# A decoder layer in split fp32: one weight transfer merged, three small steps and a row load moved earlier

## The chip, the cores and the metric

The kernel runs on one core of a Trainium2 chip. The metric is the device time of one execution in microseconds. The core has a matrix engine (TensorE; PE in the rows, PEld for its weight loads), a vector engine (VectorE, DVE), a scalar engine (ScalarE, ACT), GpSimd (POOL) and a sync engine (SP) that issues most transfers. Each engine works through its own list of instructions in order; semaphores tie the lists together.

## The reference, cut to what matters

One layer of a decoder trunk on x of 512 tokens by 1024 channels, float32: a half-step feed-forward network, a mixer, and a second half-step feed-forward network. Each reads a normalised x and adds a normalised result back to it.

```python
def swiglu(x, w_gu, w_down):
    gate, up = jnp.split(x @ w_gu, 2, axis=-1)
    return (jax.nn.silu(gate) * up) @ w_down

x = x + 0.5 * rms_norm(swiglu(rms_norm(x, ffn1_pre_g[l]), ffn1_w_gu[l], ffn1_w_down[l]), ffn1_post_g[l])
y = hybrid_mixer(rms_norm(x, mix_pre_g[l]), ...)
x = x + rms_norm(y, mix_post_g[l])
x = x + 0.5 * rms_norm(swiglu(rms_norm(x, ffn2_pre_g[l]), ffn2_w_gu[l], ffn2_w_down[l]), ffn2_post_g[l])
```

The hidden width of a feed-forward network is 2816, that is 22 chunks of 128. The mixer runs a gated linear recurrence beside sliding-window attention; the change does not touch it.

## The kernel before, in words

**Split numbers.** Every product is done with a high and a low part of each operand. ScalarE casts the high part (names with `hi`, `hh`, `xh`, "cast" below), VectorE subtracts it from the original to get the low part (`lo`, `hl`, `xl`). Three matmuls (high by high, high by low, low by high) then stand for one. So each weight that TensorE uses first costs a transfer, a cast on ScalarE and a subtraction on VectorE.

**Weights.** `Weights` (object `W`) holds two lists in program order: raw transfers into 5 buffers (`NRAW`), and units (a cast and a low part). `W.take(ahead)` hands out the next unit and first calls `fill(1 + ahead)`, which makes sure that many units are cast and split; `W.cast(n)` only casts ahead. When the last unit of a raw buffer is split, the next transfer of the list is issued on SP's queue. So where `fill` and `cast` stand in the program is where their instructions stand in ScalarE's and VectorE's lists. Casts go into 6 buffers (`NWS`). `W.later(n, fn)` runs `fn` when n more units have been taken; `W.owed` puts loads of x in the place of weight loads.

**A feed-forward network.** The first chunks are done plainly (`classic`), the others in groups of four by a scheme with seven products instead of eight (`octo`: forms `b11`, `t3`, `t2`, `b21`, `t1`, `t4`, `b22`; `SevenDown` for the way back, which also runs seven products, from `a11` to `s1`). After a group its hidden values are moved from one layout to another by 32 small transfers, half on SP's queue and half on POOL's (`place`, `ha<-sqa` and `hb<-sqb` in the rows). FFN1 works on groups from chunk 4 to 19 and has chunks 20 and 21 left; FFN2 on groups from chunk 2 to 21. Partial sums go to memory (`yp_a`, `yp_b`) and are read back in the last group.

**The end of a network.** The last group's way back is done by blocks of 128 tokens (`Last`, tb 0 to 3): TensorE finishes the two 512-column halves (dh 0 and 1) of a block, VectorE adds the partial sums (the columns of dh 1 have the negative sign), ScalarE sums the squares. In FFN1 `boundary` then normalises the rows of block after block (`Rows`: `inverse` for root and reciprocal, `x_rows` for the new x, `xn` for the normalised row), transposes them on TensorE (`tp_r`), and starts the first products of the mixer (`an`) before the last block is through. The mixer's end and the start of FFN2 go through the same function (products `mn`). In FFN2's end the sum times the post-norm gain (`grow`, a row of 1024 broadcast to 128 partitions) is done on POOL for blocks 0 to 2, and VectorE finishes with a scale and an add of x (L1971) and SP writes out.

**Order of the work around the change.** `add_layer` lists the weight transfers; `last_order` gives those of the last group and the chunks left over, by (chunk, count, dh). In `boundary` ScalarE's list holds, before block 3 is handled, a first cast, a `W.fill(2)`, then the row steps of block 2 and 3, then `W.cast(4)`. At FFN2's start ScalarE's list holds the forms of the normalised x (`n2.forms`: sums on VectorE, casts on ScalarE, low parts on VectorE), then the gates of the two plain chunks (`hid.classic`: Silu, product, split), then the units of the first way back (`bd`), which `first_part` uses. The broadcast load of `grow` is issued on SP's queue after everything of the last group, the moves of hidden blocks among it. Small tiles of 2 KB a partition (`t2k`) share 41 buffers, so a load into one can have to wait until an earlier tile is done with.

Of the kernel before, what the change touches and what calls it, by code (L numbers as in the profile page):

```python
# [11 lines left out]
AF = mybir.ActivationFunctionType  # L12
# [3 lines left out]
P = 128  # L16
T = 512
NB = T // P
D = 1024
# [15 lines left out]
OCTO1, OCTO2 = (4, 20), (2, 22)  # L35
# [86 lines left out]
def tile_layer(ctx: ExitStack, tc: tile.TileContext, out: bass.AP, **ins: bass.AP):  # L122
# [15 lines left out]
    HALF_D = [slice(0, T), slice(T, D)]  # L138
# [21 lines left out]
    W = Weights()  # L160
    w1, w2, w_in, w_o = ins["ffn1_w_gu"], ins["ffn2_w_gu"], ins["w_in"], ins["w_o"]

    def load_raw(srcs, nk, w, name):
        raw = wpool.tile([P, nk * w], F32, tag="raw", name=f"raw_{name}", bufs=NRAW).rearrange("p (k c) -> p k c", k=nk)
        o = 0
        for src in srcs:
            n = src.shape[1]
            sync.dma_start(raw[:, :, o:o + n], src.rearrange("(k p) c -> p k c", p=P))
            o += n
        return raw  # L170
# [5 lines left out]
    def add_unit(r, part, nk, c, name, low=dve, negative=False):  # L176
        def two(t, like):
            return t.rearrange("p k (i d) -> p k i d", i=2) if len(like.shape) == 4 else t

        def cast(raw):  # L180
            x, (hi, lo) = part(raw), w_tiles(nk, c, name)
            if negative:
                act.activation(hi, x, AF.Copy, scale=-1.0)
            else:
                act.copy(two(hi, x), x)
            return hi, lo

        def take_low(raw, hi, lo):
            x = part(raw)
            if negative:  # L190
                dve.scalar_tensor_tensor(lo, x, -1.0, hi.bitcast(F32), op0=ALU.mult, op1=ALU.subtract)
                return
            low.tensor_sub(two(lo, x), x, two(hi.bitcast(F32), x))

        W.unit(r, cast, take_low)
# [122 lines left out]
    def add_down(wd, name, f, n, dh, negative=False):  # L318

        down_units(down_raw(wd, name, f, n, dh), name, f, n, dh, negative)  # L320
# [8 lines left out]
    def add_layer(w_gu, wd, name, classic, octo, done):  # L329

        groups = list(range(*octo, 4))
        for f in range(done, classic, 2):
            add_gate_up(w_gu, f, name)
        if classic == octo[0] and classic == CLASSIC1:
            for dh in range(2):
                add_down(wd, name, 0, classic, dh)
        for f in groups:
            if f == groups[-1]:
                for q in range(octo[1], FC, 2):
                    add_quad(w_gu, q, name)  # L340
            add_octo(w_gu, f, name, f < CLASSIC1 and (lambda: add_downs(wd, name, 0, 2)))
            if f > groups[0]:
                add_seven_down(wd, f - 4, name)
        for f, n, dh in last_order(groups[-1], FC):
            add_down(wd, name, f, n, dh, dh)

    for add in add_pair([w1[0, :, o + P:o + 2 * P] for o in (0, F)], KD, "second", (dve, pool)):
        add()
# [49 lines left out]
    for i in range(2):  # L398
        load_x(0, i)
        for o in (0, F):  # L400
            r = first_raw[o, i] = t2k(f"first{o}{i}").rearrange("p (k c) -> p k c", k=4)
# [36 lines left out]
    def preload(func):  # L438
        act.activation(dummy, eps, func)
# [222 lines left out]
    def row_pieces(gain):  # L662
        grow = [t2k(f"grow_{gain}{dh}") for dh in range(2)]
        for dh in range(2):
            sync.dma_start(grow[dh], ins[gain][0:1, dh * T:(dh + 1) * T].to_broadcast([P, T]))
        return grow
# [71 lines left out]
    def boundary(rows, produce, parts, turns, fills, ahead, name, beside=None):  # L738


        nxt = rows.nxt
        lower, upper = range(4), range(4, KD)
        chain = iter(())

        def advance(n):
            for _ in range(n):
                next(chain, None)

        for tb in range(NB - 1):
            for dh in range(2):  # L750
                ps = produce(tb, dh)
                for t in turns.get((tb, dh), ()):
                    rows.turn(t)
                if dh == 0:
                    advance(3)
                rows.piece(tb, dh, ps, parts and parts[tb, dh])
                W.fill(fills.get((tb, dh), 0))
            chain = rows.steps(tb)
            if tb < NB - 2:
                advance(ahead)  # L760
        ps = [produce(NB - 1, dh) for dh in range(2)]
        advance(1)
        rows.turned(nxt.high, 0, lower)
        advance(1)
        rows.turned(nxt.low, 0, lower)
        W.cast(1)
        rows.turned(nxt.high, 0, upper)
        advance(1)
        rows.turned(nxt.low, 0, upper)
        W.fill(2)  # L770
        advance(1)
        for dh in range(2):
            rows.piece(NB - 1, dh, ps[dh], parts and parts[NB - 1, dh])
        if nxt.xg:
            rows.turned(nxt.keep, 0, range(KD))
        xs, (l, r) = nxt.xs, (lambda t: nxt.half(t, 0), lambda t: nxt.half(t, 1))
        W.cast(4)
        ws, banks = [], []

        def one(n, part, xpart, stop=False):  # L780
            for w, b in zip(ws[n:], banks[n:]):
                for k in range(KD):
                    pe.matmul(l(b), w[part][:, k, :], l(xs[k][xpart]), start=k + part + xpart == 0, stop=stop and k == KD - 1)  # L783

        def more():
            ws.extend(W.take(0) for _ in range(2))
            banks.extend(bank(f"{name}n{len(banks)}") for _ in range(2))

        more()
        one(0, 0, 0)  # L790
        one(0, 0, 1)
        one(0, 1, 0, True)
        chain = rows.steps(NB - 1)
        advance(4)
        W.fill(2)
        rows.turn(2)
        more()
        one(2, 0, 0)
        one(2, 0, 1)
        rows.turn(3)  # L800
        for cs in (lower, upper):
            rows.turned(nxt.high, 1, cs)
            rows.turned(nxt.low, 1, cs)
        if nxt.xg:
            rows.turned(nxt.keep, 1, range(KD))
        one(2, 1, 0, True)
        W.fill(2)
        if beside:
            beside()
        k_high(ws, banks, xs, r, range(KD))  # L810
        k_low(ws, banks, xs, r)
        return banks
# [379 lines left out]
    banks = [bank(f"a_first{i}") for i in range(4)]  # L1192
# [127 lines left out]
    hid = Hidden("a", n1)  # L1320

    def hbm_parts(name):
        return {(tb, dh): hbm.tile([P, T], F32, name=f"yp_{name}{tb}{dh}") for tb in range(NB) for dh in range(2)}
# [39 lines left out]
    def octos(hid, f0, f1, in_hbm, early=None, beside=None):  # L1363

        order = ("a11", "+s3", "s3", "a12", "+s1", "+s2", "s2", "+s4", "s4")
        parts = {}
        for f in range(f0, f1, 4):
            last = f == f1 - 4
            if last:
                for q in range(f1, FC, 2):  # L1370
                    hid.quad(q, False, AHEAD)
                W.later(11, lambda: parts.update(read_parts(hid.name, in_hbm)))
                if beside:
                    W.later(13, beside)
            if f > f0:
                down = SevenDown(hid, f - 4)
                down.ahead(zip((6, 6, 7, 8, 9, 9, 10, 11, 12) if f == f0 + 4 else (1, 2, 3, 4, 5, 6, 7, 8, 9), order))
            hid.octo(f, None if f > f0 else early)
            if f == f0:
                placed(hid, (1, 2, 3, 4))  # L1380
                continue
            if last:
                whole = Whole(hid, f)
                placed(hid, (1, 1, 2, 2), (0, 2, 1, 3))
                for n, name in zip((6, 7), ("a11", "a12")):
                    W.later(n, whole.split, name)
            else:
                placed(hid, (3, 4, 5, 6))
            kept = down.run(by_tokens, lambda half, dh, i: (parts if last else in_hbm)[2 * half + i, dh], [["a22"], ["s1"]], last)
        return whole, parts, kept  # L1390
# [71 lines left out]
    def beside():  # L1462
        grow1.extend(row_pieces("ffn1_post_g"))
        load_gates()

    whole, parts, kept = octos(hid, *OCTO1, parts1, None, beside)
# [386 lines left out]
    n2 = Turned("f2", "ffn2_pre_g", True)  # L1853
# [53 lines left out]
            wo_product(tb, dh, k0, False, k0 == 2)  # L1907
        return wo_banks[tb][dh]

    banks = boundary(rows2, produce, None, {(2, 0): [0], (2, 1): [1]}, {(0, 0): 2, (1, 0): 2}, 2, "m", n2.forms)  # L1910
    x_rows.clear()

    hid = Hidden("b", n2)
    parts2 = hbm_parts("b")
    hs = hid.classic(2, banks, {})

    def first_part():
# [4 lines left out]
        W.later(8, n2.blocks)  # L1922

    f0, f1 = OCTO2[1] - 4, FC
    whole, parts, kept = octos(hid, *OCTO2, parts2, first_part)
    hs = whole.hs
    for i in range(2):
        load_rows(i, x_hbm, pool)
    preload(AF.Sqrt)
    grow = row_pieces("ffn2_post_g")  # L1930

    last = Last(f0, f1)
    for tb in range(NB):
        end = tb == NB - 1
        pieces = [(0, 0, T)] + ([(1, 0, T // 2), (1, T // 2, T)] if end else [(1, 0, T)])
        banks = [kept.get((tb, i)) or bank(f"ybl{tb}{i}") for i in range(len(pieces))]
# [64 lines left out]
```

## Time and profile before

| | |
|---|---|
| median of 3 runs | 835.74 us (834.51 to 838.97) |
| profiled execution | 837.13 us |
| its span in the trace | 835.4 us |
| granted TensorE clock, mean | 0.997 |
| TensorE busy | 819.9 us, 98% of the span |
| VectorE / ScalarE / POOL busy | 710.1 / 541.0 / 235.6 us |
| moved by DMA | 133.22 MB, mean 159 GB/s |

Times in rows are microseconds from the start of the span: start, duration, engine, line of the kernel, operation, output<-inputs, sizes, count; in square brackets the idle time of that engine just before, and what ended it. A row with a count over 1 stands for several instructions in succession, and its duration for all of them. A matmul's duration in the rows is its way through the array; the next one starts 0.227 later where nothing holds it (512 columns). FFN1 fills the span to about 346, the mixer to about 499, FFN2 the rest; the last matmul starts at 824.68.

### The profile page before, as it was taken

The numbers are of one execution on the slowest core, as the hardware profiler recorded it, in microseconds if no ns is written. First come the engines' busy times: TensorE is split into PE (matmuls) and PEld (weight loads), VectorE is DVE, ScalarE is ACT, GpSimd is POOL, SyncE is SP. The second block draws the span as 40 slices with busy tenths as digits, with TensorE's granted clock in tenths as the row PEclk, the third lists the DMA queues.
The fourth block names the chain that finished last, engine by engine and source line by source line (L and its number), as shares of the span: only waits on it lengthen the run. The fifth ranks groups of instructions, "written<-read, shape, count | busy, mean of one in ns | idle before, by whom it ended". The sixth has DMA issues, their size and how long they took to land.

```text
span 835.4 us, 12062 instructions
## 1 busy us (share of the span) xinstructions
PE 819.9 (98%) x4156; PEld 692.2 (83%) x4156; DVE 710.1 (85%) x963; ACT 541.0 (65%) x905; POOL 235.6 (28%) x331
## 2 busy tenths in 40 slices
PE   8999999999999999999999999999999999999994
PEld 8988888888898887898788889888888888888884
DVE  4888889988979976777889777889999898889956
ACT  6756756675667564758856867865667576576642
POOL 2022004180360262005113021120327045065162
PEclk9999999999999999999999999999999999999998
DMA  8355326499594867113051453471749769499382
GB/s 253 102 185 205 128 87 187 124 208 264 131 234 111 268 147 233 51 51 102 1 102 52 166 186 126 176 224 55 224 103 218 237 168 223 139 218 251 124 206 109
DMA packets 90978, 133.22 MB, mean 159 GB/s; under 512 B 10601, under 2 KB 40613, under 8 KB 90917
## 3 DMA queue, kind: packets, MB, share of 16 engines
q1 hardware_dynamic: 69460, 91.41, 33.9%
q0 software_dynamic: 21312, 40.92, 23.0%
q8 instruction: 32, 0.52, 0.3%
q14 instruction: 30, 0.24, 0.1%
q10 hardware_dynamic: 144, 0.13, 0.0%
HBM read 93.10 MB, written 26.74 MB: 143 GB/s over the span
## 4 chain that ended last, share of the span: by engine, by line
PE 38%; DVE 9%; ACT 9%; issue 2%; DMA 1%; POOL 1%; DVEq 0%; ACTq 0%; POOLq 0%
PE ab L938 12%; PE db L938 7%; PE bb L938 3%; PE yab L1338 1%; PE yab L1339 1%; DMA x_rows<-x_hbm 1%; PE yab L1340 1%; PE wo L1871 1%; PE mn L783 1%; PE an L481 1%; ACT sc L1604 1%; PE ydb L1338 1%; PE ydb L1340 1%; PE ydb L1339 1%; PE an L783 1%
## 5 line engine op out<-in xcount | busy, mean ns | idle before, releaser
L1109 POOL DMA_DIRECT2D yp_b<-stage x46 | 44.7, 1309 | 95.1 <-ACT stage L1106 93.4
L995 POOL DMA_DIRECT2D hb<-sqb x80 | 48.2, 701 | 59.6 <-PE db L938 35.0
L995 POOL DMA_DIRECT2D ha<-sqa x64 | 38.8, 706 | 52.9 <-DVE sqa L953 44.4
L1109 POOL DMA_DIRECT2D yp_a<-stage x32 | 31.3, 1287 | 61.6 <-ACT stage L1106 60.7
L938 PE MATMUL aa<-whi_a_p,b_a 128*128 128x512 f32 x64 | 19.7, 389 | 0.0
L938 PE MATMUL ab<-whi_b_p,b_f 128*128 128x512 f32 x64 | 19.7, 389 | 0.0
L1622 POOL TENSOR_SCALAR_AFFINE_SELECT pc<-pa 128x384 f32<-128x384 f32 x8 | 5.6, 716 | 44.3 <-ACT pa L1621 43.6
L1534 POOL TENSOR_TENSOR xcl<-xc,xch 128x512 fp32r<-128x512 f32 x4 | 5.1, 1296 | 44.6 <-ACT xch L1533 44.6
L1949 ACT ACTIVATE ysq<-yp_b 128x512 f32<-128x512 f32 (+1 forms) x9 | 5.2, 582 | 16.9 <-DVE yp_b L1948 14.3
L938 PE MATMUL db<-whi_b_q,t13h_f 128*128 128x512 f32 x40 | 15.6, 389 | 0.0
L938 PE MATMUL db<-whi_b_q,t13l_f 128*128 128x512 f32 x40 | 15.6, 389 | 0.0
L938 PE MATMUL db<-wlo_b_q,t13h_f 128*128 128x512 f32 x40 | 15.6, 389 | 0.0
L938 PE MATMUL ab<-whi_b_r,t24h_f 128*128 128x512 f32 x40 | 15.6, 389 | 0.0
L938 PE MATMUL ab<-whi_b_r,t24l_f 128*128 128x512 f32 x40 | 15.6, 389 | 0.0
L938 PE MATMUL ab<-wlo_b_r,t24h_f 128*128 128x512 f32 x40 | 15.6, 389 | 0.0
L938 PE MATMUL bb<-whi_b_s,xh_f 128*128 128x512 f32 x40 | 15.6, 389 | 0.0
L938 PE MATMUL bb<-whi_b_s,xl_f 128*128 128x512 f32 x40 | 15.6, 389 | 0.0
L938 PE MATMUL bb<-wlo_b_s,xh_f 128*128 128x512 f32 x40 | 15.6, 389 | 0.0
L938 PE MATMUL ab<-whi_b_t,t13h_f 128*128 128x512 f32 x40 | 15.6, 389 | 0.0
L938 PE MATMUL ab<-whi_b_t,t13l_f 128*128 128x512 f32 x40 | 15.6, 389 | 0.0
L938 PE MATMUL ab<-wlo_b_t,t13h_f 128*128 128x512 f32 x40 | 15.6, 389 | 0.0
L938 PE MATMUL db<-whi_b_u,t24h_f 128*128 128x512 f32 x40 | 15.6, 389 | 0.0
(1538 smaller groups left out, 3275.7 us busy)
## 6 DMA issues: line engine op xcount, KB each, us to landing
yp_b<-stage POOLq DMA_DIRECT2D x54, 256.0 KB, 6.2
yp_a<-stage POOLq DMA_DIRECT2D x40, 256.0 KB, 6.4
raw_ad<-in_ffn_w_down SPq DMA_DIRECT2D x4, 1024.0 KB
hb<-sqb SPq DMA_DIRECT2D x80, 32.0 KB, 4.2
hb<-sqb POOLq DMA_DIRECT2D x80, 32.0 KB, 4.2
xn<-in_x SPq DMA_DIRECT2D x8, 256.0 KB, 3.2
ha<-sqa SPq DMA_DIRECT2D x64, 32.0 KB, 3.7
ha<-sqa POOLq DMA_DIRECT2D x64, 32.0 KB, 3.7
```

What stands on the lines that cost most here:

```text
L481: pe.matmul(sl(ps), w[:, k, :], xh, start=False, stop=False, skip_group_check=True)
L783: pe.matmul(l(b), w[part][:, k, :], l(xs[k][xpart]), start=k + part + xpart == 0, stop=stop and k == KD - 1)
L938: pe.matmul(o, x, w[:, k, :], start=first and i + k + j == 0, stop=i == 1 and k == 1 and j == 2, skip_group_check=True)
L995: (sync if i else pool).dma_start(o, squares[rows, 8 * pair + q:8 * pair + q + 5:4].rearrange("f c b t -> f c (b t)"))
L1109: pool.dma_start(o, st, accum_op=ALU.add)
L1338: pe.matmul(banks[i], hh[:, js], hi[:, k, :], start=first and k == 0, stop=False, skip_group_check=True)
L1339: pe.matmul(banks[i], hh[:, js], lo[:, k, :], start=False, stop=False, skip_group_check=True)
L1340: pe.matmul(banks[i], hl_[:, js], hi[:, k, :], start=False, stop=k == 1, skip_group_check=True)
L1604: act.activation(sc[:, b * P:(b + 1) * P], blocks[b], AF.Exp, bias=nm[:, b:b + 1], scale=scale, accum_out=den[:, b:b + 1])
L1622: pool.affine_select(v4(pc)[:, 1:, :], v4(pa)[:, 1:, :], pattern=[[0, NB - 1], [1, P]], base=0, channel_multiplier=-1, compare_op=ALU.is_g ...
L1871: pe.matmul(wo_banks[tb][dh], x, w[:, k, :], start=start and k == 0 and w is hi and not xp, stop=stop and k == 1 and xp == 1, skip_group_c ...
L1949: act.activation(wt(f"ysq{tb}{i}")[:, :c1 - c0], y, AF.Square, accum_out=ss[:, i:i + 1])
```

## The change

It does five things in four places. (1) The weights of FFN1's chunks 20 and 21 on the way back, two transfers of 0.5 MB (one for each half of the columns), become one transfer of 1 MB with two units. FFN2 has no such chunks left, so its list stays. (2) In `boundary`, for FFN1 only, the casts of the third and fourth unit are issued before the last row step of block 2 instead of after the sums of block 3. (3) In FFN2 a preload of the Silu table stands ahead of the forms, (4) and `W.fill(3)` puts one more unit (the first of `bd`) ahead of the gates and splits of the plain chunks. (5) FFN2's post-norm row is loaded by the hook of the last group, 13 units after its start, as FFN1's row already is, instead of after the group.

```diff
         for f, n, dh in last_order(groups[-1], FC):
-            add_down(wd, name, f, n, dh, dh)
+            if n == 4:
+                add_down(wd, name, f, n, dh, dh)
+                continue
+            if not dh:
+                r = W.raw(lambda f=f, n=n: load_raw([wd[0, f * P:(f + n) * P]], n, D, f"{name}d{f}"))
+            add_unit(r, lambda raw, dh=dh: raw[:, :, HALF_D[dh]], n, T, f"{name}d{f}{dh}", negative=dh)
...
         rows.turned(nxt.low, 0, upper)
         W.fill(2)
+        if parts:
+            W.cast(4)
         advance(1)
...
-    banks = boundary(rows2, produce, None, {(2, 0): [0], (2, 1): [1]}, {(0, 0): 2, (1, 0): 2}, 2, "m", n2.forms)
+    def beside():
+        preload(AF.Silu)
+        n2.forms()
+
+    banks = boundary(rows2, produce, None, {(2, 0): [0], (2, 1): [1]}, {(0, 0): 2, (1, 0): 2}, 2, "m", beside)
     x_rows.clear()
 
     hid = Hidden("b", n2)
     parts2 = hbm_parts("b")
+    W.fill(3)
     hs = hid.classic(2, banks, {})
...
-    whole, parts, kept = octos(hid, *OCTO2, parts2, first_part)
+    grow = []
+    whole, parts, kept = octos(hid, *OCTO2, parts2, first_part, lambda: grow.extend(row_pieces("ffn2_post_g")))
     hs = whole.hs
     for i in range(2):
         load_rows(i, x_hbm, pool)
     preload(AF.Sqrt)
-    grow = row_pieces("ffn2_post_g")
```

## The prediction

> **What bounds the kernel now.** I read the page's busy line first, then the waits of TensorE alone, then the timelines of each engine around every wait found, and last the timelines of the final 35 us. The page's line, and below it the three of TensorE's waits that lie where the change does (engine, line, releaser: us in total, times, longest):
>
> ```profile
> PE 819.9 (98%) x4156; PEld 692.2 (83%) x4156; DVE 710.1 (85%) x963; ACT 541.0 (65%) x905; POOL 235.6 (28%) x331
> ```
> ```profile
> PE yea L1329 <- DVE wlo_ad L191: 0.8, 1, 0.8
> PE yb L1329 <- DVE wlo_bd L193: 0.4, 1, 0.4
> PE an L783 <- ACT whi_xl L185: 0.4, 1, 0.4
> ```
>
> TensorE is busy for 819.9 of 835.4 us, so the kernel is bound by it except for a handful of holes and for the stretch after its last product. The change touches exactly the three holes shown and that stretch. As TensorE sets the pace in between, a hole that closes moves everything behind it forward; the question is by how much, and whether the next late thing is close behind. Whatever the change brings is therefore a sum of small pieces, some us of 835.
>
> **Part 1: weights of FFN1's chunks 20 and 21 in one transfer.** Before, the second half of these weights (output columns 512 on) is a load of its own, which stands on SP's queue behind 16 block moves of the hidden state. Here are SP's loads, ScalarE's cast, and TensorE around the hole:
>
> ```profile
> 270.33 8.17 SPq L168 DMA_DIRECT2D raw_ad<-in_ffn_w_down  x3
> ...
> 308.52 0.62 SPq L168 DMA_DIRECT2D raw_ad<-in_ffn_w_down  x1
> ```
> ```profile
> 315.99 1.06 ACT L183 ACTIVATE whi_ad<-raw_ad 128x1024 fp32r<-128x1024 f32 x1 [5.37 <-DMA raw_ad<-in_ffn_w_down]
> ```
> ```profile
> 316.58 0.39 PE L1330 MATMUL yba<-whi_ad,hla 128*128 128x512 f32 x1
> ...
> 318.36 0.50 PE L1329 MATMUL yea<-wlo_ad,hha 128*128 128x512 f32 x1 [0.76 <-DVE wlo_ad L191]
> ...
> 319.63 0.39 PE L1328 MATMUL yba<-whi_ad,hha11a 128*128 128x512 f32 x1
> ```
>
> The load goes out at 308.52, lands 7.47 us later (315.99), and the cast, then the low part on VectorE, come just too late. Merged, it goes out with the third of the three loads that SP issues from 270.33 to 278.5, with 0.5 MB more. ScalarE is idle for 5.37 us before the late cast, that is from 310.62; the cast then ends at 311.7 and the low part near 313.4 instead of 318.3. TensorE wants them from 316.8, so there are 3 us to spare. The hole is larger than the 0.76 shown, because the product before it waited too and the pipeline refills: from the last undisturbed start (316.58) to the first of the next block (319.63) lie seven steps that take 0.227 each when nothing waits, 1.59, and they took 3.05. Gone are **1.46 us** at most. Next late is the low part of block a21, wanted by TensorE at 319.63 + 38 x 0.227 = 328.25:
>
> ```profile
> 327.37 0.69 DVE L1404 TENSOR_TENSOR hla21a<-ha,hha21a 128x512 fp32r<-128x512 f32 x1 [0.78 <-ACT hha21a L1403]
> ```
>
> It is done at 328.06, 0.2 us ahead. It hangs on the chain of block 0, which starts from the same late bank, so it moves too, though ScalarE puts the two casts of the gate weights into that chain, which move by a little less. I take 1.4; bounds 0.2 (the chain doesn't move) and 1.46. The weight loads behind on SP's queue (two of w_in, the keys and values) each go out one place earlier; that costs nothing, since their buffers free in the same order.
>
> **Part 2: two casts ahead of the rows in FFN1's boundary.** ScalarE's queue, then TensorE's and VectorE's:
>
> ```profile
> 348.35 0.73 ACT L721 ACTIVATE xn_r<-x_rows,rs1x_r 128x512 f32<-128x512 f32 x1 [2.22 <-DVE rs1x_r L687]
> ...
> 352.01 1.99 ACT L185 CAST whi_xl<-raw_xl__3174 128x1024 fp32r<-128x1024 f32 x2
> ```
> ```profile
> 351.69 1.04 PE L732 MATMUL tp_r<-ident,xn_r 128*128 128x128 f32 x8
> 353.10 2.17 PE L783 MATMUL an<-xh_mx,whi_xl 128*128 128x256 f32 x16 [0.37 <-ACT whi_xl L185]
> ...
> 357.03 1.04 PE L732 MATMUL tp_r<-ident,xn_r 128*128 128x128 f32 x8
> 357.82 2.20 PE L783 MATMUL an<-xh_mx,wlo_xl 128*128 128x256 f32 x16
> ```
> ```profile
> 356.39 2.35 DVE L193 TENSOR_TENSOR wlo_xl<-raw_xl__3174,whi_xl 128x1024 fp32r<-128x1024 f32 x2
> ```
>
> The two casts (1.99) move from 352.01 into the 2.22 us in which ScalarE waits for VectorE before xn_r, from 346.13: they fit. Were that cover gone, xn_r would come up to 1.99 later, at 351.07, still before its transposes at 351.69. TensorE's gap after the transposes was 353.10 - 351.69 = 1.41 where the next one took 0.79: **0.62 us** go. What is late next is the two low parts: the second ends at 358.74, TensorE reaches it about 358.8. The rows of block 3 start their squares about 0.5 us earlier once the casts aren't ahead of them, so the low parts come earlier by about that on top of part 1, a little less than the 0.62. I take 0.45; bounds 0 and 0.62.
>
> **Part 3: the Silu table and one unit ahead of FFN2's first gates.** ScalarE, VectorE, TensorE:
>
> ```profile
> 521.43 0.63 ACT L630 CAST t13h_f<-ta_f 128x512 fp32r<-128x512 f32 x1 [3.29 <-DVE ta_f L626]
> ...
> 524.33 1.28 ACT L825 ACT_TABLE_LOAD   x1
> ...
> 528.11 2.00 ACT L185 CAST whi_bd<-raw_bd 128x1024 fp32r<-128x1024 f32 x2
> ```
> ```profile
> 525.38 0.68 DVE L638 TENSOR_TENSOR t24l_f<-tb_f,t24h_f 128x512 fp32r<-128x512 f32 x1
> ...
> 529.19 2.36 DVE L193 TENSOR_TENSOR wlo_bd<-raw_bd,whi_bd 128x1024 fp32r<-128x1024 f32 x2 [0.26 <-ACT whi_bd L185]
> ```
> ```profile
> 529.66 0.39 PE L1328 MATMUL yb<-whi_bd,hhb 128*128 128x512 f32 x1
> 530.47 0.50 PE L1329 MATMUL yb<-wlo_bd,hhb 128*128 128x512 f32 x1 [0.43 <-DVE wlo_bd L193]
> ...
> 531.04 0.39 PE L1328 MATMUL yb<-whi_bd,hhb 128*128 128x512 f32 x1
> ```
>
> The table load (1.28, plus a dummy activation) moves ahead of the forms, into the 3.29 us in which ScalarE waits for VectorE: no cost. The cast of the first down unit (1.0 of the 2.00) takes its place, and its low part (1.18 of the 2.36) runs on VectorE from 526.06, when the forms end, to 527.25 instead of 529.19 to 530.4. That pushes the gate product on VectorE, then the split, back by about 1.0: ScalarE's copies, done when it turned to whi_bd at 528.11, end near 529.1, still before TensorE asks at 529.66. Without that 0.5 us the hole would return as a wait for the split. The steps 529.66 to 531.04 took 1.38 where three take 0.68: **0.70 us** go; bounds 0 and 0.70, and I take 0.7.
>
> **Part 4: the post-norm row during the last group.** Two broadcast loads move on SP's queue from behind the last 16 block moves to ahead of them. The tail, by SP and POOL, ScalarE, VectorE:
>
> ```profile
> 802.06 2.53 SPq L665 DMA_DIRECT2D grow_ffn_post_g<-in_ffn_post_g  x2
> ```
> ```profile
> 812.10 1.29 POOL L1956 TENSOR_TENSOR yp_b<-yp_b,grow_ffn_post_g 128x512 f32<-128x512 f32 x1 [7.35 <-DMA grow_ffn_post_g<-in_ffn_post_g]
> 814.08 1.29 POOL L1956 TENSOR_TENSOR yp_b<-yp_b,grow_ffn_post_g 128x512 f32<-128x512 f32 x1 [0.69 <-DMA grow_ffn_post_g<-in_ffn_post_g]
> ```
> ```profile
> 809.25 0.63 ACT L1949 ACTIVATE ysq<-yp_b 128x512 f32<-128x512 f32 x1 [1.99 <-DVE yp_b L1946]
> ```
> ```profile
> 810.52 0.69 DVE L1404 TENSOR_TENSOR hla21b<-hb,hha21b 128x512 fp32r<-128x512 f32 x1 [1.30 <-ACT hha21b L1403]
> ...
> 812.33 1.08 DVE L1964 TENSOR_TENSOR tot_b<-ss_b 128x1 f32<-128x1 f32 x1
> ...
> 814.04 2.54 DVE L1971 SCALAR_TENSOR_TENSOR yp_b<-yp_b,rs_b,x_rows 128x512 f32<-128x512 f32 x2
> 816.50 0.68 DVE L1948 TENSOR_TENSOR yp_b<-ybb,yp_b 128x512 f32<-128x512 f32 x1
> ...
> 826.91 0.68 DVE L1948 TENSOR_TENSOR yp_b<-ydb,yp_b 128x512 f32<-128x512 f32 x1
> ...
> 830.08 0.16 DVE L1962 TENSOR_TENSOR tot_b<-tot_b,ss_b 128x1 f32<-128x1 f32 x1 [0.18 <-ACT ysq L1949]
> ```
>
> Block 0's products on POOL wait 7.35 and 0.69 us for the row, and VectorE's two final steps take 2.54 because they need them. Block 1's add at 816.50 and block 3's at 826.91 carry no idle mark: VectorE is late against TensorE, and each block takes 5.2 us (10.41 for two), so what block 0 gains goes through to the end. With the row at hand POOL's second product runs as soon as its squares are read, near 810.0 to 811.3, and the final steps need nothing but tot_b. Undisturbed that add takes 0.16 (the row at 830.08), ends at 812.5, and after 0.63 for root and reciprocal (813.41 to 814.04 today) and 1.4 for two steps of about the add's 0.68 block 1 starts at 814.55: 1.95 gained. But the add at 812.33 took 1.08 and ended at 813.41, just when POOL's product did (812.10 + 1.29): an add that reads twice from SBUF stood still beside POOL. Moved to 810.0, the product would do the same to hla21b: held to 811.3 instead of starting at 810.52, 0.8 later. So 1.95 - 0.8 = **1.15** is what I take, as the trace shows the hold; bounds 0 and 1.95.
>
> The Trainium skill, "SBUF — State Buffer", section "Who interferes with whom", has the same as a rule: a VectorE instruction with two SBUF inputs contends with a GpSimd instruction that reads SBUF, and the loser blocks for the whole instruction. It speaks against part of this gain; by it the tail yields the 1.15, without it 1.95, and the row of 1.08 agrees with it.
>
> On SP's queue the rows now stand ahead of the block moves; the moves wait for VectorE until 789.85, and FFN1's own row, loaded at the same place of its last group, shows how long such a load waits for a buffer (SP's waits between 270 and 320):
>
> ```profile
> SPq L665 <- PE aa L938: 1.8, 1, 1.8
> ```
> ```profile
> 789.85 12.11 SPq L995 DMA_DIRECT2D hb<-sqb  x16
> ```
> ```profile
> 799.25 0.69 DVE L1404 TENSOR_TENSOR hla11b<-hb,hha11b 128x512 fp32r<-128x512 f32 x1 [1.52 <-DMA hb<-sqb]
> ```
> ```profile
> 803.34 0.39 PE L1330 MATMUL ybb<-whi_bd,hla11b 128*128 128x512 f32 x1
> ```
>
> With a wait of that size SP is through with the row, which is issued in the last group's products, well before VectorE lets the block moves go, so I cost it at nothing; the moves have another 803.34 - 799.94 = 3.4 us before TensorE notices.
>
> **The sum.** 1.4 + 0.45 + 0.7 + 1.15 = 3.7 us. The profiled execution took 837.13 (span 835.4), so 833.4 in its terms; the median of the three runs is 835.74, 1.39 lower, and gives **832.0**, 0.45% less.
>
> **Rivals.** *The hole moves instead of closing* (FFN1's end): if block 0's chain doesn't start earlier, TensorE stops at hla21a after 0.2 us. For it: the slack of 0.2; against: that chain begins at the very bank that was late. 0.2 + 0.45 + 0.7 + 1.15 = 2.5: 833.2. *The tail doesn't move*: the row of x from memory, or the hold by POOL falling on more than hla21b, sets block 0's end; for it the 1.08, against it that VectorE had nothing else to wait for at 814. 2.55 remain: 833.2. *The change takes effect in full*, without the hold and without new waits: 1.46 + 0.62 + 0.7 + 1.95 = 4.73: 831.0. *Slower*: the two early row buffers are not free, and SP stands still with the block moves behind it. If it stood until 802.06, where the rows go out today, the moves would be 12.2 late, TensorE 8.8 after its slack; less 3.7, +5.1: 840.8. It decides from 3.4 + 3.7 = 7.1 us, that is a hold beyond 797.0. Against it: FFN1's wait of 1.8 at the same place.
>
> **How the numbers follow.** Forecast (near 832.0, between 831.5 and 832.7) 0.45; in full (831.0) 0.19; hole moves 0.14; tail doesn't move 0.16; slower 0.06. About 0.5%, 4.2 us or 831.56, is what a measurement of this kernel can tell from no change; the runs shown reach from 1.2 under to 3.2 over their median. Faster by more than that: the full case and about two fifths of the forecast, with scatter, 0.37; slower 0.05; the rest, 0.58, within. The range goes from the full case less the runs' scatter (830.0) to the two smaller gains with the same on top (834.5).
>
> **What would show it.** FFN1: no late load of raw_ad near 308, no wait of yea. Boundary: the two whi_xl casts before xn_r, no wait of an. FFN2: the table load near 518, the cast of whi_bd before the gates, no wait of yb. Tail: rows out some us ahead of the block moves, POOL's products right behind their squares, block 1's add about 1.2 earlier against TensorE. I am wrong if a new wait on hla21a, wlo_xl or the split appears, or block moves start after 789.85 by TensorE's clock.

## The result, and the profile after

The changed kernel takes **833.27 us** (median of 8 executions, 832.09 to 833.53) against 835.65 for the kernel before on the same chip (8 executions, 834.51 to 839.28): ratio 0.9961, 95% interval 0.9944 to 0.9978, so 0.39% less. The profiled executions stand at 833.29 and 837.13, their spans at 831.6 and 835.4. The forecast was 832.0 us, 0.45% less.

Of the changed kernel first the page's span and busy line, then the whole answer to TensorE's waits (engine, line, releaser: us in total, times, longest), then the page's line of the chain of work that ended last, by engine:

```profile
span 831.6 us, 12057 instructions
...
PE 819.1 (98%) x4156; PEld 692.4 (83%) x4156; DVE 708.6 (85%) x963; ACT 540.1 (65%) x906; POOL 235.1 (28%) x331
```
```profile
PE warm L1191 <- POOL ident masks.py:199: 1.4, 1, 1.4
PE a_first L486 <- ACT xh_a L537: 0.7, 1, 0.7
PE xtp L1138 <- DMA xn<-in_x: 0.6, 2, 0.4
PE tp_r L737 <- DVE xn_r L728: 0.3, 1, 0.3
```
```profile
PE 83%; ACT 6%; DVE 5%; DMA 2%; issue 1%; POOL 1%; SPq 0%; DVEq 0%; ACTq 0%; POOLq 0%
```

TensorE did the same work; its waits for yea, yb and an are gone, and no new one stands in the list. In the kernel before, the chain that ended last lay on TensorE for 38% of the span; now for 83%.

TensorE's starts at the four places are these (changed kernel, timeline of TensorE; lines have moved by 5 to 12 against the kernel before):

```profile
318.17 0.39 PE L1335 MATMUL yba<-whi_ad,hha11a 128*128 128x512 f32 x1
...
326.89 0.50 PE L1337 MATMUL yda<-whi_ad,hla21a 128*128 128x512 f32 x1
...
344.69 2.08 PE L790 MATMUL an<-xh_mx,whi_xl 128*128 128x256 f32 x16
...
351.23 2.15 PE L790 MATMUL an<-xh_mx,whi_xl 128*128 128x256 f32 x16
...
527.77 0.39 PE L1335 MATMUL yb<-whi_bd,hhb 128*128 128x512 f32 x1
528.45 0.39 PE L1335 MATMUL yb<-whi_bd,hhb 128*128 128x512 f32 x1
...
822.09 0.28 PE L1337 MATMUL ybl<-whi_bd,hla22b 128*128 128x256 f32 x1
```

Against the kernel before, block 1's first step comes 1.46 earlier (319.63), and the first an 1.25 (345.94): 0.21 was lost on the way. The second an is 1.87 earlier (353.10), the fourth yb step 2.59 (531.04), and the last matmul still 2.59 (824.68): nothing is given back in FFN2. The tail, by VectorE and POOL:

```profile
807.92 1.38 DVE L1411 TENSOR_TENSOR hla21b<-hb,hha21b 128x512 fp32r<-128x512 f32 x1 [1.30 <-ACT hha21b L1410]
...
810.43 0.15 DVE L1976 TENSOR_TENSOR tot_b<-ss_b 128x1 f32<-128x1 f32 x1
...
812.53 0.69 DVE L1960 TENSOR_TENSOR yp_b<-ybb,yp_b 128x512 f32<-128x512 f32 x1
...
822.96 0.68 DVE L1960 TENSOR_TENSOR yp_b<-ydb,yp_b 128x512 f32<-128x512 f32 x1
```
```profile
804.75 1.29 POOL L1968 TENSOR_TENSOR yp_b<-yp_b,grow_ffn_post_g 128x512 f32<-128x512 f32 x1 [2.63 <-ACT ysq L1961]
807.46 1.30 POOL L1968 TENSOR_TENSOR yp_b<-yp_b,grow_ffn_post_g 128x512 f32<-128x512 f32 x1 [1.42 <-ACT ysq L1961]
```

POOL's products now run behind their squares. Block 1's add is 3.97 earlier (816.50), that is 1.38 beyond TensorE's 2.59. To compare executions I use its lead on the last matmul: 816.50 - 824.68 = -8.18 before, 812.53 - 822.09 = **-9.56** after. So the profiled executions differ by 1.25 + 0.62 - 0.05 + 0.07 + 0.70 + 1.38 = 3.97 at block 1's add (the 0.07 come in small pieces between 360 and 524), and the spans by 3.8. The medians differ by 2.4. That gap between one execution and the median is what the experiments are about.

### The profile page after: what moved, and what is told of

It reads as the page before. It is cut to its first block, busy times and chain, and to the rows that moved or that the text cites. A ratio compares the mean times of both kernels' runs of the same rounds, so it can differ in the third digit from the quotient of the medians.

```text
span 831.6 us, 12057 instructions
## 1 busy us (share of the span) xinstructions
PE 819.1 (98%) x4156; PEld 692.4 (83%) x4156; DVE 708.6 (85%) x963; ACT 540.1 (65%) x906; POOL 235.1 (28%) x331
## 4 chain that ended last, share of the span: by engine, by line
PE 83%; ACT 6%; DVE 5%; DMA 2%; issue 1%; POOL 1%; SPq 0%; DVEq 0%; ACTq 0%; POOLq 0%
PE ab L945 13%; PE aa L945 10%; PE db L945 7%; PE da L945 5%; PE bb L945 3%; PE ba L945 3%; PE an L790 1%; PE aa L885 1%; PE mn L790 1%; PE wo L1878 1%; DMA x_rows<-x_hbm 1%; DMA raw_second<-in_ffn_w_gu 1%; PE yab L1346 1%; PE yab L1345 1%; PE yab L1347 1%
## 5 line engine op out<-in xcount | busy, mean ns | idle before, releaser
L945 PE MATMUL db<-wlo_b_u,t24h_f 128*128 128x512 f32 x40 | 15.6, 389 | 0.0
L945 PE MATMUL db<-whi_b_u,t24l_f 128*128 128x512 f32 x40 | 15.6, 389 | 0.0
L945 PE MATMUL ab<-whi_b_v,xh_f 128*128 128x512 f32 x40 | 15.6, 389 | 0.0
L945 PE MATMUL ab<-wlo_b_v,xh_f 128*128 128x512 f32 x40 | 15.6, 389 | 0.0
```

Of the source, the lines that this page charges most:

```text
L945: pe.matmul(o, x, w[:, k, :], start=first and i + k + j == 0, stop=i == 1 and k == 1 and j == 2, skip_group_check=True)
```

## The experiments

The theory: four separate gains that add up, of which two, the late weight load and the late row, depend on when a transfer lands, so that one profiled execution doesn't give their size. Times of the kernel before are those taken in the same series; the series ran on different chips (e1 to e4 on one, f0, f1, e8 and e9 on another, g1, g2 and e0 on a third, f2 on a fourth).

### Each part alone

From the kernel before, with one hunk of the diff each:

```diff
 e1_merge:      the hunk in add_layer (one transfer, two units)
 e2_casts:      + if parts: W.cast(4)
 e3_silu_fill:  + preload(AF.Silu) ahead of n2.forms(), + W.fill(3)
 e4_row:        grow loaded by the hook of the last group
```

> Kernel before with the merged transfer alone. Theory (the gains are four separate holes): no wait of yea; first yba of block 1 near 318.2 (before 319.63), first an near 344.7 (345.94), still 0.2 lost at hla21a; everything behind keeps that 1.25, the last matmul near 823.4 (824.68), and the span is 834.1 to 834.2. Rival A (the hole moves): first an within 0.3 of 345.9 and the last matmul within 0.3 of 824.7. Rival B (the late landing of the load was an accident of the one profiled execution of before): the medians of the two kernels do not differ, though the profile shows the hole gone.

> Kernel before with the two earlier casts in FFN1's boundary alone. Theory: everything up to the first an at 345.94 as before, the second an 0.6 earlier (353.10 to 352.5), the last matmul near 824.1, span 834.8; the wait of yea stays. Rival (the casts only fit because the merged transfer had moved the rows too): the wait of an stays or turns into one of tp_r or wlo_xl, the last matmul within 0.2 of 824.68.

> Kernel before with the Silu table and the unit ahead of FFN2's first gates alone. Theory: identical up to 524, no wait of yb, the fourth yb step 0.70 earlier (531.04 to 530.34), last matmul near 824.0, span 834.7. Rival (given back later in FFN2, where a move or a weight is late): last matmul within 0.2 of 824.68.

> Kernel before with the early row alone. Theory: TensorE as before to the end (last matmul 824.68 within 0.1), block 1's add 1.4 earlier (816.50 to 815.1), block 0's second product on POOL holds one low part on VectorE to 1.4 instead of 0.69, the sum of the squares takes 0.16 instead of 1.08; span 834.0 to 834.1. Rival (the tail gained only because TensorE's holes had closed): block 1's add within 0.3 of 816.5, span 835.1 or more.

| | executions | median, us | range | at 837 or above | ratio to before, 95% |
|---|---|---|---|---|---|
| before | 35 | 835.10 | 833.49 to 843.02 | 8 | |
| e1_merge | 12 | 833.90 | 833.51 to 834.73 | 0 | 0.9974 (0.9955 to 0.9994) |
| e2_casts | 12 | 834.54 | 833.59 to 838.60 | 1 | 0.9982 (0.9961 to 1.0004) |
| e3_silu_fill | 12 | 834.93 | 833.41 to 839.76 | 5 | 0.9996 (0.9971 to 1.0021) |
| e4_row | 12 | 834.57 | 833.27 to 839.17 | 3 | 0.9984 (0.9961 to 1.0007) |

By the times, the merged transfer is the only part that can be told from no change, and with it the long executions are gone. The traces say more. The two fixed parts are as expected: in e2 the second an follows the first after 353.97 - 347.42 = 6.55 instead of 7.16, **0.61** less, and in e3 the four yb steps take 529.35 - 528.67 = 0.68 instead of 1.38, **0.70** less, with 293.64 from there to the last matmul in both kernels. But the parts that were not changed moved too. Here are the late load on SP, its cast on ScalarE, and TensorE, in e2 and then in e4, which both have it unchanged:

```profile
307.47 0.65 SPq L168 DMA_DIRECT2D raw_ad<-in_ffn_w_down  x1
```
```profile
317.41 1.06 ACT L183 ACTIVATE whi_ad<-raw_ad 128x1024 fp32r<-128x1024 f32 x1 [7.66 <-DMA raw_ad<-in_ffn_w_down]
```
```profile
318.52 0.49 PE L1330 MATMUL yea<-whi_ad,hha 128*128 128x512 f32 x1 [2.41 <-ACT whi_ad L183]
```
```profile
308.31 0.39 SPq L168 DMA_DIRECT2D raw_ad<-in_ffn_w_down  x1
```
```profile
314.51 1.06 ACT L183 ACTIVATE whi_ad<-raw_ad 128x1024 fp32r<-128x1024 f32 x1 [3.96 <-DMA raw_ad<-in_ffn_w_down]
```
```profile
316.73 0.39 PE L1328 MATMUL yea<-whi_ad,hha 128*128 128x512 f32 x1
```

The same 0.5 MB landed 9.94 us after its issue in e2 and 6.20 in e4, where TensorE didn't wait at all (the bracket is missing). The row did the same: block 1's add leads by -9.08 in e1 and by -9.56 in e2 and e3, though all three load it late. In e3 POOL's product ran behind its squares with the late row:

```profile
799.09 1.28 SPq L665 DMA_DIRECT2D grow_ffn_post_g<-in_ffn_post_g  x2
```
```profile
808.36 1.29 POOL L1961 TENSOR_TENSOR yp_b<-yp_b,grow_ffn_post_g 128x512 f32<-128x512 f32 x1 [1.42 <-ACT ysq L1954]
```

So e1's tail, which was to stay, gained 0.90 more of a lead on the last matmul, and e2's hole at yea grew from 1.46 to 3.76. Of the four spans (832.9, 834.9, 832.4, 832.7) only e2's is the one expected, and that by accident. Where TensorE starts on the last group differs too: the same step, the first of yea with hha11a, lies between 311.68 and 313.11 in the fourteen profiles, at 312.73 and 311.95 in the two of the kernel before. e4's add leads by -9.56 as expected.

### The changed kernel again, and less its merged transfer

f0_after is the changed kernel; f1_no_merge has the lines of `add_layer` as they were before:

```diff
 for f, n, dh in last_order(groups[-1], FC):
-    if n == 4: ...        # and the one transfer with two units
+    add_down(wd, name, f, n, dh, dh)
```

> The changed kernel once more. Theory (two of its four gains close holes whose size differs from execution to execution): no wait of yea or yb, only starts of the first 14 us differ; all executions within about 1.5 us of each other, none at 837 or above, median 833.0 to 833.5, while the kernel before has about a quarter of its executions at 837 and above. Rival (the long executions are the chip's and not the kernel's): the changed kernel has them as often, 3 of 12.

> The changed kernel without the merged transfer (chunks 20 and 21 in two transfers again). Theory: the wait of yea returns, between 0 and 4 us by when the load lands (6.2 us after issue: none; 7.5: 1.5; 9.9: 3.8); median 0 to 1.3 above the changed kernel, 2 to 5 of 12 executions at 837 or above, where the changed kernel has none. Rival A (1.25 us lost in every execution): median 1.2 above, no long executions. Rival B (part 1 brings nothing): median and spread as the changed kernel.

f0: median 833.06 (12 executions, 832.27 to 834.04), ratio 0.9961 (0.9943 to 0.9979), no wait of yea, none at 837 or above, where the kernel before had 15 of 32 in this series. f1: median 834.56 (832.67 to 840.45), 4 of 12 at 837 or above. So part 1 is worth 1.50 us of the median in this series and, by the means (835.62 and 833.05), 2.57. The median lies a little above the expected 0 to 1.3; the long executions are as expected, and both rivals fall. The changed kernel's executions lie 1.77 apart, a little more than the 1.5 expected. f1's own profile is its shortest execution, and shows 0.56 lost at yea.

### The tail's order, and the gate weights

e8_tail_splits moves three instructions of FFN2's end, e9_gates four of FFN1's:

```diff
 e8:  ahead of block 0's first add:
+    for name in ("a21", "a22"): whole.split(name)
+    kept["late"]()
 (and not after its products)
 e9:  if (tb, dh) == (0, 1): split_gates()      removed
+     in (1, 0), behind the splits of a21, a22:  split_gates()
```

> The changed kernel with the two low parts a21, a22 and the late sum moved ahead of block 0's first add, into the 2.03 us in which VectorE waits there. Theory (the tail is set by VectorE's order, and POOL's second product holds whatever reads twice from SBUF beside it): hla21b back to 0.69, block 1's add relative to the last matmul 1.6 to 2.3 earlier (-9.56 to -11.2 or -11.9), span 829.3 to 830.0, median 1.6 to 2.3 below the changed kernel. Which end: 1.6 if POOL's product also holds the sum of the squares (1.4 instead of 0.15), 2.3 if that gets in first. Rival (the tail is set by something behind block 0, by ScalarE's squares or the write-out): under 0.5 less.

> The changed kernel with the gate weights' split (two casts on ScalarE, two low parts on POOL) moved in FFN1's end from block 0 to behind the low parts a21, a22 in block 1. Theory (these four instructions hold block 0's chain: 0.5 on ScalarE ahead of the second squares, 0.8 on VectorE, whose x steps take 2.25 beside POOL instead of 1.42): hla21a ends about 1.3 earlier, the 0.21 lost there by TensorE is gone, first an 344.69 to 344.5, span 0.2 less; medians do not differ measurably. Rival (the hold falls on block 1 instead, on zr or the sums of squares there): a wait of tp_r before the first an, which comes later than 344.69.

e8: median **831.54** (9 executions, 830.82 to 833.10), 1.52 below f0 in the same series, just short of the 1.6 to 2.3 expected; span 829.9. VectorE in e8:

```profile
801.27 0.69 DVE L1411 TENSOR_TENSOR hla21b<-hb,hha21b 128x512 fp32r<-128x512 f32 x1
804.48 0.69 DVE L1411 TENSOR_TENSOR hla22b<-hb,hha22b 128x512 fp32r<-128x512 f32 x1 [2.52 <-ACT hha22b L1410]
...
805.69 0.68 DVE L1964 TENSOR_TENSOR yp_b<-ybb,yp_b 128x512 f32<-128x512 f32 x1
...
807.77 0.74 DVE L1976 TENSOR_TENSOR tot_b<-ss_b 128x1 f32<-128x1 f32 x1 [0.81 <-ACT ysq L1965]
...
810.89 0.68 DVE L1964 TENSOR_TENSOR yp_b<-ybb,yp_b 128x512 f32<-128x512 f32 x1
```

Away from POOL's product hla21b is back to 0.69; block 1's add leads the last matmul (822.26) by -11.37, 1.81 better. With the row early, the tail was set by VectorE's order. A wait that I had not foreseen held the first add: the cast of a22 stood until 803.83 for a block move.

e9: median 833.26 against 833.06, not to be told apart. hla21a starts 6.78 after block 1's first step instead of 7.97, and the first an follows it after 26.31 instead of 26.52: the **0.21** that part 1 lost at hla21a is gone, as expected. VectorE's x steps of block 0 in the kernel before, in the changed kernel and in e9:

```profile
322.29 2.25 DVE L711 SCALAR_TENSOR_TENSOR x_rows<-zr,rs1y_r,x_rows 128x512 f32<-128x512 f32 x2
```
```profile
321.07 2.25 DVE L716 SCALAR_TENSOR_TENSOR x_rows<-zr,rs1y_r,x_rows 128x512 f32<-128x512 f32 x2
```
```profile
320.58 1.41 DVE L716 SCALAR_TENSOR_TENSOR x_rows<-zr,rs1y_r,x_rows 128x512 f32<-128x512 f32 x2
...
327.35 1.73 DVE L708 TENSOR_TENSOR zr<-yp_a,grow_ffn_post_g 128x512 f32<-128x512 f32 x1
```

The hold beside POOL's low parts left the x steps of block 0 (2.25 to 1.41) and fell on a product of block 1 (1.73 where it takes 0.69), where nobody waits. The edit moves ScalarE's two casts and POOL's two low parts together, so it doesn't part their shares.

### What makes the load late, and the kernel before once more

g1_x_late is the kernel before with the second load of x in FFN1's end (two transfers of 0.5 MB on POOL's queue) held back; g2_tail_gates joins e9 and a better order than e8's; e0_before is the kernel before.

```diff
 g1:  in (0, 1), behind split_gates():
+     for o, src in held: pool.dma_start(o, src)    # x_rows 2 and 3
 g2:  e9's edit, and in FFN2's block 0:
+     whole.split("a21")       ahead of the first add
+     kept["late"]()           between the two adds
+     cast of a22 behind the first squares, low part behind the second add
```

> The kernel before (two transfers for chunks 20 and 21) with the second load of x in FFN1's end (two transfers of 0.5 MB on POOL's queue, 307.95 in the kernel before, 0.6 us ahead of the late weight load) held back until block 0's gate weights are split, some 322. Theory (the load goes out at about 308.5 in every execution and lands 6.2 to 9.9 us later because the DMA engines are full, share 1.0 from 308 to 320, above all with that x): it lands within 6 us, the wait of yea goes, first yba of block 1 at 318.2 to 318.4, and executions at 837 or above, 8 of 35 and 16 of 32 in the kernel before, are gone or rare (0 or 1 of 12); median 1 to 2 below the kernel before. Rival A (the 32 small block moves ahead of it hold the load, x does not): lands 6 to 10 us after issue as before, long executions as often as in the kernel before. Rival B (the long executions have another place): the wait of yea is gone but long executions stay.

> The changed kernel with the gate weights' split moved as in e9, and in FFN2's end only a21 split ahead of block 0's first add, the late sum between block 0's two adds, a22 cast behind the first squares and split behind the second add. Theory (VectorE's order sets the tail; in e8 the cast of a22 waited for a block move until 803.83 and held the first add to 805.69 instead of 803.4): first add near 803.4 by e8's clock, the sum of the squares 0.2 earlier than in e8, POOL's second product off the final steps (1.42 instead of 1.82), block 1's add 0.2 to 0.5 earlier relative to the last matmul (-11.37 to between -11.6 and -11.9), with the gates 0.2 more from hla21a; span 829.2 to 829.6, median 0.4 to 0.7 below e8. Rival (the tail is now set by TensorE and by the fixed end of block 3): block 1's add earlier, but the span only by the 0.2 of the gates.

> The kernel before, one look. Theory (the wait of yea and the lateness of the post-norm row differ by execution): first yba of block 1 between 318.1 and 324, with the landing of raw_ad 6 to 12 us after its issue, and block 1's add 8.2 to 9.6 ahead of the last matmul; an execution above 837 shows a wait of yea of 3 us or more. Rival: the same holes as in the first profile within 0.2 us (1.46 and 8.18).

By the times it was 15 of 32, not the 16 in the text of g1. **e0** took 838.29. Its timelines of SP, ScalarE, TensorE and VectorE:

```profile
307.89 0.62 SPq L168 DMA_DIRECT2D raw_ad<-in_ffn_w_down  x1
```
```profile
317.76 1.06 ACT L183 ACTIVATE whi_ad<-raw_ad 128x1024 fp32r<-128x1024 f32 x1 [7.92 <-DMA raw_ad<-in_ffn_w_down]
```
```profile
314.68 0.39 PE L1328 MATMUL yba<-whi_ad,hha 128*128 128x512 f32 x1
...
318.87 0.49 PE L1328 MATMUL yea<-whi_ad,hha 128*128 128x512 f32 x1 [2.67 <-ACT whi_ad L183]
...
321.39 0.40 PE L1328 MATMUL yba<-whi_ad,hha11a 128*128 128x512 f32 x1
```
```profile
816.71 0.75 DVE L1971 SCALAR_TENSOR_TENSOR yp_b<-yp_b,rs_b,x_rows 128x512 f32<-128x512 f32 x1 [1.18 <-POOL yp_b L1956]
817.38 0.68 DVE L1948 TENSOR_TENSOR yp_b<-ybb,yp_b 128x512 f32<-128x512 f32 x1
```

Landed 9.87 after issue; the twelve steps from 314.68 to 321.39 took 6.71 instead of 2.72, so **3.99** were lost where the first profile of the same program lost 1.46. The add leads the last matmul (826.35) by -8.97, where it led by -8.18. The rival of equal holes falls. Over the seven profiles with the separate load (last column: how long before it POOL issued the second load of x, two transfers of 0.5 MB):

| | landed after, us | lost by TensorE at yea, us | x issued ahead by, us |
|---|---|---|---|
| e4 | 6.20 | 0.04 | 0.03 |
| g1 | 6.39 | 0.20 | held back |
| f1 | 7.24 | 0.56 | 0.49 |
| e3 | 7.26 | 1.19 | 0.55 |
| before | 7.47 | 1.46 | 0.57 |
| e0 | 9.87 | 3.99 | 0.64 |
| e2 | 9.94 | 3.76 | 0.59 |

POOL's issue of that x in the kernel before as first profiled (load at 308.52), then in e4 (load at 308.31):

```profile
307.95 1.80 POOL L1456 DMA_DIRECT2D x_rows<-in_x  x2
```
```profile
308.28 1.80 POOL L1456 DMA_DIRECT2D x_rows<-in_x  x2
```

The load's stretch in e0, by two microseconds (after the window its length, busy us of PE, PEld, DVE, ACT and POOL, then the granted clock, the busy share of the DMA engines, GB/s):

```profile
308.00:310.00 2.00, 2.00 (x11) 1.65 (x10) 1.64 (x3) 1.81 (x3) 1.64 (x4) 1.00 1.15 177
...
316.00:318.00 2.00, 0.20 (x1) 0.00 (x0) 0.00 (x0) 0.24 (x1) 0.00 (x0) 1.00 1.03 246
```

The DMA engines are nearly full from the issue to the landing (0.89 to 1.15 in the five stretches). **g1** takes 1 MB out of that time: the load landed after 6.39, not within the 6 expected, the hole was 0.20, and no execution of 11 reached 837 (highest 836.96; before 4 of 15, so that chance alone would do this about once in eleven times). Its median, 835.60, is not below the 835.36 of before, where 1 to 2 were expected: that half of the expectation failed. Its one profile is of a short execution (834.27) and doesn't show what the others lose; x held back may cost elsewhere. g1's landing alone proves nothing, since e4's was as early with x in place. But in e4 x went out only 0.03 us ahead of the load, and in the five with the later landings 0.49 to 0.64. So the profiles fit with an x that has got in ahead and delays the load; what makes it 7.3 in one and 9.9 in another is open.

**g2**: median **830.28** (5 executions, 830.11 to 831.27), ratio to before 0.9947 (0.9934 to 0.9959), span 829.4 as expected. VectorE:

```profile
802.96 0.69 DVE L1961 TENSOR_TENSOR yp_b<-ybb,yp_b 128x512 f32<-128x512 f32 x1 [1.43 <-PE ybb L1337]
...
807.16 0.16 DVE L1979 TENSOR_TENSOR tot_b<-ss_b 128x1 f32<-128x1 f32 x1 [0.19 <-ACT ysq L1964]
...
809.62 0.68 DVE L1961 TENSOR_TENSOR yp_b<-ybb,yp_b 128x512 f32<-128x512 f32 x1
811.12 0.69 DVE L1959 SCALAR_TENSOR_TENSOR yp_b<-yp_b,yeb 128x512 f32<-128x512 f32 x1 [0.82 <-PE yeb L1337]
```

Block 1's add leads the last matmul (821.83) by -12.21, 0.84 better than e8 and more than the 0.2 to 0.5 expected. VectorE now waits for TensorE in block 1 (0.82), so the end gains less: the last three steps start 2.60 after the last matmul (824.43), in e8 2.93 (825.19). The spans of g2 and e8 differ by 0.5, and the last matmul alone is 0.43 earlier in g2, so that the profiles don't exclude the rival; the medians differ by 1.26, but on two chips. This version beats both kernels.

### The changed kernel less its early row

```diff
-whole, parts, kept = octos(..., first_part, lambda: grow.extend(row_pieces("ffn2_post_g")))
+whole, parts, kept = octos(..., first_part)
 ...
+grow = row_pieces("ffn2_post_g")       # behind preload(AF.Sqrt), as before
```

> The changed kernel without the early row (the post-norm row again issued behind the block moves of the last group). Theory (the row's landing differs by execution: block 1's add stood 8.18, 8.97, 9.08, 9.21, 9.56 and 9.56 ahead of the last matmul in the six executions profiled with the late row, 9.56 in all with the early one and the old order of VectorE): add between 8.2 and 9.6 ahead, TensorE's waits as in the changed kernel, median 0.2 to 0.8 above the changed kernel's 833.06 to 833.27, no execution at 837 or above. Rival A (1.38 in every execution, as in the first comparison): median 1.4 above, some 834.5. Rival B (the early row brings nothing outside the one execution): median as the changed kernel, within 0.2.

Median 833.70 (12 executions, 832.77 to 835.18), 0.4 to 0.6 above the changed kernel's two medians, which were taken on other chips; none at 837 or above. The profiled execution had the row in time (-9.56). So the row's lateness is a matter of the execution: 1.38, 0.59, 0.48, 0.35, 0, 0 and 0 in the seven profiles with the late row (before, e0, e1, g1, e2, e3, f2). Rival A falls; rival B does by the traces, while a difference of 0.4 to 0.6 across chips doesn't show it by the times.

The lateness goes with SP's issues ahead of the row. SP in e1 and in e3 (e3's row is shown above):

```profile
788.16 12.12 SPq L1000 DMA_DIRECT2D hb<-sqb  x16
800.37 2.36 SPq L670 DMA_DIRECT2D grow_ffn_post_g<-in_ffn_post_g  x2
```
```profile
788.16 10.84 SPq L995 DMA_DIRECT2D hb<-sqb  x16
```

The sixteen block moves took SP 11.86 to 12.12 us in the four profiles with a late row, and 10.76 to 10.85 in the three with the row in time. Why SP's issues differ is not shown.

## Why the prediction was right, and where it wasn't

**The sum, in its own terms.** The profiled execution was to come to 833.4 and came to 833.29. In it the likeliest case occurred: all three holes close, the tail moves, POOL's product holds hla21b. That it agrees to 0.1 is partly luck: the terms are off by up to 0.23 both ways, and another execution of the kernel before, e0, took 838.29 with a hole of 3.99. By the terms: **part 1** 1.4, measured 1.25. The hole of 1.46 is wholly gone; the named next in line, hla21a, took 0.21 back, since its chain moved by 1.23 (326.14 against 327.37). The prediction hung that chain on the late bank. It begins with the add of block 0's first half, which in the kernel before stood on VectorE behind the late low part:

```profile
318.23 0.68 DVE L696 TENSOR_TENSOR yp_a<-yba,yp_a 128x512 f32<-128x512 f32 x1
```
```profile
317.01 0.69 DVE L701 TENSOR_TENSOR yp_a<-yba,yp_a 128x512 f32<-128x512 f32 x1 [3.71 <-PE yba L1337]
```

That add moved by 1.22. ScalarE then runs the first squares, the two gate casts, as said, and the second squares without a pause, so the chain moved by as much and not by 1.46. The hold of the x steps by POOL's low parts was not seen, but it is 2.25 in both kernels: it takes from the slack, not from the move. e9 removes the casts and the hold, and the 0.21 with them. **Part 2** 0.45, measured 0.57 (0.62, less 0.05 at the low parts): the next in line is there, but smaller. **Part 3** 0.7, measured 0.70. **Part 4** 1.15, measured 1.38: the hold was 0.69 instead of 0.8, and the rest of the row's chain came 0.12 sooner than worked out. The Trainium skill's rule that was weighed there ("SBUF — State Buffer", section "Who interferes with whom") agrees with the trace: hla21b took 1.38 beside POOL's product, and 0.69 in e8, where that product ran at another time.

**The step that failed** is the last one of the sum, and it put the median outside the forecast's own 831.5 to 832.7, at the 833.2 of two rivals that did not occur in the profiled execution: "the median of the three runs is 835.74, 1.39 lower, and gives **832.0**". It carried the whole 3.7 over from an execution that stood 1.39 above the median to the median itself. But part of what put that execution above its median was, by the seven profiles with the late row, what the change removes: there the row was 1.38 late, and in three of the seven it was not late at all. Sized by the medians, part 1 brings 1.50 (f1 to f0) and part 4 0.4 to 0.6 (across chips); with the fixed 0.57 and 0.70 the sum is an estimated 3.2 to 3.4. The series gave 835.65 - 833.27 = 2.4 and 836.37 - 833.06 = 3.3, the first with 2 of 8 long executions of before, the second with 15 of 32. With 3.2 to 3.4 the forecast would have been 832.3 to 832.5, so this accounts for 0.3 to 0.5 of the 1.27 by which it was low. The rest, 0.7 to 0.9, stays open; the median of before itself lies between 835.10 and 836.37 in the five series.

**What it didn't say** is the change's larger effect, on the spread. With the separate load 49 of 155 executions were at 837 or above (36 of 107 of the kernel before, 13 of 48 of e2, e3, e4 and f1); with the merged one none of 70 (highest 835.18). g1, which also keeps the load separate but holds x back, had none of 11. e0 shows where one such execution, of 838.29, loses its time. But e2's profiled execution lost about as much at yea (3.76) and took 836.64, so that this hole alone doesn't make the 31 executions of 839 to 843, none of which was profiled. In the 30 of them with a clock on record the mean granted clock was 0.988 to 0.995 (median 0.991), against 0.993 to 0.998 in those below 837, with either load. Whether the lower clock costs them time or follows from a longer wait is not shown; that they go away when the load is merged is.

**The rivals.** *The hole moves* was right about the place and wrong about the size: 0.21, not 1.2. The median is at its price, 833.2, for another reason. *The tail doesn't move* fell for the profiled execution, yet is what happens in the executions in which the row is in time anyway. *In full* fell to the hold. *Slower*: the early row went out at 767.85, the block moves at 787.25, which is 2.60 before 789.85, as TensorE is 2.59 ahead; SP waited 3.6 for the row's two buffers, where 1.8 was taken as the size, and it cost nothing:

```profile
767.85 2.15 SPq L670 DMA_DIRECT2D grow_ffn_post_g<-in_ffn_post_g  x2
...
787.25 11.92 SPq L1002 DMA_DIRECT2D hb<-sqb  x16
```

## What to carry to other kernels

The two waits here that end with a transfer have no single size. Before such a wait is priced, ask whether its length is that of every execution, and if the profiled one stands above the median, don't take the gain from the median as well. A load that lands just in time can be worth moving for the spread alone. And where a late operand is brought forward, look at what its consumer then runs beside: here the better order of VectorE (g2) gave another 2.8 us between the medians, though not taken on the same chip, which no earlier load could.

## What was not expected of the hardware

One transfer of 0.5 MB, in the same place of the same program, landed after 7.47 us in one execution and 9.87 in another, with the DMA engines' busy share between 0.89 and 1.15 from issue to landing in both. Sixteen block moves, begun at 788.16 in both e1 and e3, took SP 12.12 us in the one and 10.84 in the other. And VectorE's holds beside POOL reach well beyond the one predicted: two x steps took 2.25 instead of 1.41, a product 1.73 instead of 0.69, and the sum of two columns 0.74 in e8 where it takes 0.15. The first fell on another instruction when POOL's work was moved (e9), and the last was gone in g2.
